# Sums of the down projection's weights: formed in DRAM during gate and up instead of in SBUF during the down projection

## The chip, the cores and the metric

The kernel runs on one core of a Trainium2 chip. The metric is the device time of one execution in microseconds (us), the median of several runs.

## The reference, cut to what matters

Two layers of a diffusion backbone. 640 tokens (512 latent, 128 context) of width 1024 pass a token mixer and a dense channel mixer. The stages concerned are the channel mixer's:

```python
def swiglu(h, w_gate_up, w_down):
    g, u = jnp.split(h @ w_gate_up, 2, axis=-1)
    return (jax.nn.silu(g) * u) @ w_down
...
    h2 = rmsnorm(x, g_pre_ffn) * (1.0 + scale2) + shift2
    x = x + gate2 * rmsnorm(swiglu(h2, w_gate_up, w_down), g_post_ffn)
```

`w_gate_up` is 1024 x 5632 and `w_down` 2816 x 1024 per layer, all float32. The modulation vectors (`scale`, `shift`, `gate`) come from `silu(c) @ w_ada`.

## The kernel before, in words

Every float32 matmul is made as three matmuls of rounded parts (`mm3`, L225): an operand is split into a high part by ScalarE (L211) and a low part by VectorE (L217), and high x high, high x low and low x high are summed in PSUM. So each block of weights is loaded to a `raw` buffer (three of them, 512 KB each), split by both engines into a `w` buffer (eight of them, shared with other large tiles), and read by TensorE.

**Gate and up** (`gate_up`, L944) goes over 22 column blocks of 128 hidden channels. The first two (`plain`) are multiplied directly; for the other 20, `fast` uses seven products of a 2 x 2 scheme of Strassen's kind instead of eight, each of 4 x 3 matmuls of 320 columns. `prep` (L964), a generator, loads the next block's two halves (L969), forms four sums of quarters on VectorE and splits seven operands; one step of it is made after each product of the current block. The results stand in six `hid` tiles.

**The down projection** (`w_down`, L1045) does the same with seven products over the contraction, in the order p1, p2, p5, p6, p3, p7, p4. Each goes over six groups of hidden channels (five of two 128-row blocks, one of one), so 11 blocks per product, with three accumulators of 512 columns (p1, p2, p3, p7) or two (p5, p6, p4). One group's weights are 512 KB. With (e, h) for the quarter of the weights, p1 uses (0,0), p2 (1,0), p3 (1,1), and the others sums: p5 (0,0)+(0,1); p6 that plus (1,1); p4 that plus (1,0); p7 (0,1)+(1,1). The sums are made by transfers that add into SBUF (`add`, L1078, issued by GpSimd): p1 loads into three `wk` tiles `V` (`into`, L1073), splits, then adds (0,1); p5 splits and adds (1,1); p6 splits and adds (1,0); p4 splits. p7 loads a fresh `raw` (`fresh`, L1081), adds to it and splits:

```python
        def p7(g):
            r = fresh(g, 0, 1)
            add(r, 1, 1, g)
            w = wsplit(g, r)
```

`run` (L1108) makes the operands of group g + 1 before the matmuls of group g. Pieces of the ends of earlier products (`later`: copies of accumulators to `cc`, `finish`, `end`) are put between the groups. In p7 and p4 the last two groups are run accumulator by accumulator (`tail=2`).

**The order of the work.** The program is written as one stream; each engine and each DMA queue (SP's, GpSimd's) works through its own instructions in the order of that stream as a scheduler lays it out, and waits on semaphores. A clock `now` counts TensorE's time while the program is built: `spawn` and `part` place delayed pieces by it, and `bg` holds background steps, one each time that the interval written with it has passed (`clk`, L160). In layer 0's gate and up the background is `queue_ada_w` (L383): the next layer's first modulation, 32 VectorE steps over 8 loads of 1 MB into `wk` tiles, one every 6.6 us. In layer 1's there is none.

Of the kernel before, what the change touches and what calls it, by code (L numbers as in the profile page):

```python
# [10 lines left out]
F32 = mybir.dt.float32  # L11
R = mybir.dt.float32r
AF = mybir.ActivationFunctionType
ALU = mybir.AluOpType
# [5 lines left out]
NJ = FF // 128  # L20
NPLAIN = 2
# [110 lines left out]
class Trunk:  # L132
# [250 lines left out]
    def queue_ada_w(self, l, r):  # L383


        nc, src = self.nc, self.a["ada"][3 * l + r - 1]
        mod, mc = self.new_mod(l, r)
        order = [(half, kk) for half in range(2) for kk in range(4)]
        box, raws = {}, []

        def fetch():
            if order:
                half, kk = order.pop(0)
                raw = self.W()
                nc.sync.dma_start(out=raw[:].rearrange("p (e n) -> p e n", e=2),
                                  in_=src[2 * kk : 2 * kk + 2, :, half * 1024 : half * 1024 + 1024].rearrange("e p n -> p e n"))
                raws.append(raw)

        def step(half, k, s):
            if k == 0 and s == 0:  # L400
                box["acc"] = self.wp.tile([128, 2, 1024], F32, tag="w", name=self.nm("acc"))
            if k % 2 == 0 and s == 0:
                box["raw"] = raws.pop(0)
                fetch()
            acc, raw = box["acc"], box["raw"][:, (k % 2) * 1024 : (k % 2) * 1024 + 1024]
            c = self.cond[:, k, s : s + 1]
            if k == 0:
                nc.vector.tensor_scalar(acc[:, s], raw, c, None, op0=ALU.mult)
            else:
                nc.vector.scalar_tensor_tensor(acc[:, s], raw, c, acc[:, s], op0=ALU.mult, op1=ALU.add)  # L410
            if k == 7 and s == 1:
                self.spawn(self.ada_sum(mod, mc, half, acc, 4.0), 5.66)

        return mod, [fetch] + [lambda h=h, k=k, s=s: step(h, k, s) for h in range(2) for k in range(8) for s in range(2)]

# [528 lines left out]
    def gate_up(self, l, pre):  # L944
        nc, a, blk = self.nc, self.a, self.blk
        hid = [self.Q([4, N], F32, "hid") for i in range(NJ // 4)]

# [5 lines left out]
        def plain(j, ws, c):  # L953
# [8 lines left out]
            out(j, c, pu[:, 0:320], s[:], nc.vector)  # L962

        def prep(j, ops):  # L964

            raws = []
            for u in range(2):
                raws.append(self.raw())
                nc.sync.dma_start(out=raws[u], in_=a["w_gu"][l, j, u])  # L969
            r = [x[:].rearrange("p (k i n) -> p k i n", k=4, i=2) for x in raws]  # L970
            (a11, a21), (a12, a22) = [[x[:, :, i, :] for i in range(2)] for x in r]
            g = [self.gp.tile([128, 2, 4, 128], F32, tag="gg", name=self.nm("sw")) for _ in range(2)]
            (s1, s2), (s3, s4) = [[x[:, i] for i in range(2)] for x in g]
            sums = {1: (s1, a21, a22, ALU.add), 2: (s2, s1, a11, ALU.subtract), 3: (s4, a12, s2, ALU.subtract), 4: (s3, a11, a21, ALU.subtract)}
            w = None
            for i, s in enumerate((a11, s1, s2, s4, s3, a12, a22)):
                if i % 2 == 0:
                    w = self.wp.tile([128, 2, 2, 4, 128], R, tag="w", name=self.nm("w"))
                if i in sums:
                    self.tt(*sums[i])  # L980
                op = [w[:, x, i % 2] for x in range(2)]
                self.split(op[0], op[1], s)
                ops.append(op)
                yield

        def fast(j, ops, nxt):
# [34 lines left out]
            product(C, a12, blk[1][0], True, g11)  # L1021
            product(A, a22, t4, False, lambda: out(j, 0, A, g0, nc.vector))

        ws = [[self.load(a["w_gu"][l, j, u]) for u in range(2)] for j in range(NPLAIN)]
        self.join(*pre[:3])
        for j in range(NPLAIN):
            plain(j, ws[j], 0)
        self.join(*pre)
        self.t_sums(256, 64)
# [4 lines left out]
        for j in range(NPLAIN):  # L1034
            plain(j, ws[j], 1)
            for _ in range(8):
                next(nxt, None)
# [6 lines left out]

    def w_down(self, l, src, hid, gg, nxt):  # L1045

# [11 lines left out]
        dd = [self.Q([3, 2, 384], F32, "dd") for _ in range(2)]  # L1058
        V = [None] * 3

# [8 lines left out]

        def vg(g):  # L1070
            return V[g // 2][:, (g % 2) * 1024 : (g % 2) * 1024 + cnt(g) * 512]

        def into(g, e, h):  # L1073
            if V[g // 2] is None:
                V[g // 2] = self.W()
            nc.sync.dma_start(out=vg(g), in_=dram(e, h, g))

        def add(dst, e, h, g):  # L1078
            nc.gpsimd.dma_start(out=dst, in_=dram(e, h, g), accum_op=ALU.add)

        def fresh(g, e, h):  # L1081
            r = self.raw()[:, 0 : cnt(g) * 512]
            nc.sync.dma_start(out=r, in_=dram(e, h, g))
            return r

        def wsplit(g, s):
            w = self.wp.tile([128, 2, 1024], R, tag="w", name=self.nm("w"))
            n = cnt(g) * 512
            self.split(w[:, 0, :n], w[:, 1, :n], s)
            return w  # L1090
# [85 lines left out]
        def p1(g):  # L1176
            into(g, 0, 0)
            w = wsplit(g, vg(g))
            add(vg(g), 0, 1, g)
            h = xsplit(g, [x(g, 0)[:, :, A4]])  # L1180
            self.tt(d(g), x(g, 1)[:, :, D4], x(g, 0)[:, :, D4], ALU.subtract)
            return h, w
# [6 lines left out]
        def p2(g):  # L1189
            w = wsplit(g, fresh(g, 1, 0))  # L1190
            return xsplit(g, [x(g, 1)[:, :, A4]]), w
# [13 lines left out]
        def p5(g):  # L1205
            w = wsplit(g, vg(g))
            add(vg(g), 1, 1, g)
            return xsplit(g, [d(g)[:, :, 128:384]]), w
# [5 lines left out]
        def p6(g):  # L1214
            w = wsplit(g, vg(g))
            add(vg(g), 1, 0, g)
            s = d(g)[:, :, 128:384]
# [8 lines left out]
        def p3(g):  # L1226
            w = wsplit(g, fresh(g, 1, 1))
            s = d(g)[:, :, 128:384]
# [8 lines left out]
        def p7(g):  # L1237
            r = fresh(g, 0, 1)
            add(r, 1, 1, g)
            w = wsplit(g, r)  # L1240
            h = self.Q([2, 2, 384], R, "hs")
# [7 lines left out]
        def p4(g):  # L1249
            return xsplit(g, [x(g, 1)[:, :, B4]]), wsplit(g, vg(g))  # L1250

# [90 lines left out]
    def run(self):  # L1342
# [4 lines left out]
        for l in range(L):  # L1347
# [8 lines left out]
            pre = self.w_out(l, src, x, ys, gg, mod2, last)  # L1356
            nxt = None
            if l + 1 < L:
                mod1, q = self.queue_ada_w(l + 1, 0)
                self.bg, self.bg_last = [(6.6, f) for f in q], self.now + 12.0  # L1360
            hid = self.gate_up(l, pre)
            self.drain_bg()
            gg = self.gates(gate, 1)
            if l + 1 < L:
                h = self.new_h()
                src = self.dp.tile([NT, 128, D], F32, tag="xs", name=self.nm("xs"))
                nxt = (mod1, h, src)
            pre = self.w_down(l, x, hid, gg, nxt)
            if l + 1 < L:
# [41 lines left out]
```

## Time and profile before

| | us |
|---|---|
| median of 3 runs (1386.08 to 1392.72) | 1387.79 |
| the profiled execution's own time | 1396.39 |
| its span in the profile | 1394.5 |
| TensorE busy in the span | 1342.1 |
| VectorE busy | 1023.3 |
| ScalarE busy | 692.0 |
| GpSimd busy | 151.3 |

Busy time of TensorE counts a matmul from start to a modelled end, and matmuls overlap; the distance of the starts tells its rate better. DMA-issuing instructions are not counted as busy. The granted clock of TensorE was 0.992 of full speed over the span. In the views, PE is TensorE, DVE VectorE, ACT ScalarE, POOL GpSimd and SP the engine that issues the plain transfers; `ps` is a tile in PSUM, `hs` the split activations of the down projection.

### The profile page before, as it was taken

Reading aid. Unit: us, or ns where it says so; the run is one execution under the profiler, and the core shown is the slowest. Engines: PE = TensorE matmul, PEld = TensorE weight load, DVE = VectorE, ACT = ScalarE, POOL = GpSimd, SP = SyncE. Lnnn points to the kernel's source line nnn. Section 1 sums busy time; section 2 is a strip of 40 time slices with the busy share of each in tenths; the row PEclk is TensorE's granted clock in tenths of the full one; section 3 lists DMA queues with packets and bytes.
Section 4 is the critical chain, followed back from the end, with each engine's and each line's share of the span. In section 5 each row is a group of like instructions: output and inputs, shape, how many; then the busy total and the mean of one; then the engine's idle time right before and its main releaser. Section 6 shows DMA issues by size and latency. Waiting matters only on the chain.

```text
span 1394.5 us, 21421 instructions
## 1 busy us (share of the span) xinstructions
PE 1342.1 (96%) x8188; PEld 1206.2 (86%) x8188; DVE 1023.3 (73%) x1794; ACT 692.0 (50%) x1398; POOL 151.3 (11%) x186
## 2 busy tenths in 40 slices
PE   5899999999999999999899999999999999999996
PEld 2788977899999999888688998878999999998875
DVE  3789476499988985776788956757977777675955
ACT  4543275465554554545583324746644544444633
POOL 1101121110000000111211101302000000010220
PEclk9999999999999999999999999999999999999998
DMA  9555247244333333768655533553222322375982
GB/s 373 168 166 184 82 147 241 99 146 143 125 108 106 120 121 110 194 139 192 183 181 184 186 112 121 176 204 124 73 92 91 90 78 85 98 184 126 183 211 97
DMA packets 57974, 203.68 MB, mean 146 GB/s; under 512 B 7488, under 2 KB 8384, under 8 KB 56848
## 3 DMA queue, kind: packets, MB, share of 16 engines
q1 hardware_dynamic: 50960, 179.25, 38.7%
q0 software_dynamic: 6912, 23.07, 9.4%
q8 instruction: 64, 1.05, 0.3%
q14 instruction: 38, 0.31, 0.1%
HBM read 191.61 MB, written 10.68 MB: 145 GB/s over the span
## 4 chain that ended last, share of the span: by engine, by line
PE 71%; DMA 9%; DVE 8%; issue 5%; ACT 4%; POOL 2%; POOLq 0%; DVEq 0%; SPq 0%; ACTq 0%
PE ps L227 22%; PE ps L229 22%; PE ps L228 22%; DMA raw<-in_w_dn 4%; PE ps L240 2%; DVE w L217 2%; DVE acc L377 2%; PE ps L284 2%; ACT w L211 2%; DMA raw<-in_w_out 1%; PE ps L829 1%; POOL rt L252 1%; DMA raw<-in_ada 1%; DMA raw<-in_w_vpc 1%; DMA raw<-in_w_b 1%
## 5 line engine op out<-in xcount | busy, mean ns | idle before, releaser
L217 DVE TENSOR_TENSOR w<-raw,w 128x512 fp32r<-128x512 f32 (+2 forms) x220 | 197.5, 903 | 105.5 <-ACT w L211 104.0
L211 ACT ACTIVATE w<-raw 128x512 fp32r<-128x512 f32 (+2 forms) x220 | 175.4, 801 | 185.5 <-PE ps L229 74.8
L227 PE MATMUL ps<-T,w 128*128 128x320 f32 x640 | 198.5, 310 | 0.0
L229 PE MATMUL ps<-T,w 128*128 128x320 f32 x640 | 197.8, 309 | 0.0
L228 PE MATMUL ps<-T,w 128*128 128x320 f32 x640 | 197.7, 309 | 0.0
L227 PE MATMUL ps<-b,w 128*128 128x320 f32 x608 | 188.1, 309 | 0.0
L228 PE MATMUL ps<-b,w 128*128 128x320 f32 x608 | 187.9, 309 | 0.0
L229 PE MATMUL ps<-b,w 128*128 128x320 f32 x608 | 187.9, 309 | 0.0
L227 PE MATMUL ps<-w,hs 128*128 128x512 f32 x396 | 156.7, 396 | 6.6 <-ACT cc L211 4.6
L229 PE MATMUL ps<-w,hs 128*128 128x512 f32 x396 | 156.4, 395 | 5.5 <-DVE hs L217 5.4
L228 PE MATMUL ps<-w,hs 128*128 128x512 f32 x396 | 156.3, 395 | 0.2 <-DVE w L217 0.2
L211 ACT ACTIVATE w<-sw 128x512 fp32r<-128x512 f32 x160 | 96.3, 625 | 77.3 <-PE ps L229 65.3
L211 ACT ACTIVATE s<-ps 128x320 f32<-128x320 f32 (+2 forms) x148 | 65.3, 443 | 129.1 <-PE ps L229 105.9
L214 DVE TENSOR_TENSOR s<-ps,s 128x320 f32<-128x320 f32 (+1 forms) x144 | 68.7, 482 | 80.1 <-PE ps L229 79.9
L227 PEld LDWEIGHTS ps<-T,w 128*128 128x128 f32 x640 | 120.1, 188 | 2.1 <-issue 1.7
L228 PEld LDWEIGHTS ps<-T,w 128*128 128x128 f32 x640 | 120.1, 188 | 0.0
L229 PEld LDWEIGHTS ps<-T,w 128*128 128x128 f32 x640 | 120.1, 188 | 0.0
L227 PEld LDWEIGHTS ps<-b,w 128*128 128x128 f32 x608 | 114.1, 188 | 0.4 <-ACT s L211 0.3
L228 PEld LDWEIGHTS ps<-b,w 128*128 128x128 f32 x608 | 114.1, 188 | 0.1
L229 PEld LDWEIGHTS ps<-b,w 128*128 128x128 f32 x608 | 114.1, 188 | 0.0
L217 DVE TENSOR_TENSOR w<-sw,w 128x512 fp32r<-128x512 f32 x160 | 106.2, 686 | 5.1 <-ACT w L211 3.1
L227 PEld LDWEIGHTS ps<-w,hs 128*128 128x128 f32 x396 | 75.6, 191 | 23.8 <-ACT cc L211 5.4
(236 smaller groups left out, 2856.3 us busy)
## 6 DMA issues: line engine op xcount, KB each, us to landing
raw<-in_w_gu SPq DMA_DIRECT2D x88, 512.0 KB, 3.5
raw<-in_ada SPq DMA_DIRECT2D x64, 512.0 KB, 4.3
raw<-in_w_dn SPq DMA_DIRECT2D x30, 512.0 KB, 4.3
wk<-in_w_dn POOLq DMA_DIRECT2D x30, 512.0 KB, 6.2
ada<-in_ada SPq DMA_DIRECT2D x8, 1024.0 KB, 15.5
raw<-in_w_out SPq DMA_DIRECT2D x16, 512.0 KB, 4.1
wk<-in_ada SPq DMA_DIRECT2D x8, 1024.0 KB
xs<-work SPq DMA_DIRECT2D x15, 512.0 KB, 4.6
```

Source lines behind the costliest of these rows:

```text
L211: self.nc.scalar.activation(out, in_, f, **kw)
L214: self.nc.vector.tensor_tensor(out, x, y, op=op)
L217: self.nc.vector.tensor_tensor(lo, src, hi.bitcast(F32), op=ALU.subtract)
L227: mm(out, lh, rh, start=start, stop=False, skip_group_check=more)
L228: mm(out, lh, rl, start=False, stop=False, skip_group_check=more)
L229: mm(out, ll, rh, start=False, stop=stop, skip_group_check=more)
L240: self.nc.tensor.transpose(out, in_, self.ident)
L252: self.nc.gpsimd.tensor_tensor(r2, r, self.mhalf[:, :n], op=ALU.pow)
L284: self.nc.tensor.matmul(ps[32 * j : 32 * j + 32, :], self.cond[:, k, :], s, start=start, stop=stop, tile_position=(0, 32 * j))
L377: nc.vector.scalar_tensor_tensor(acc[:, s], raw, c, acc[:, s], op0=ALU.mult, op1=ALU.add)
L829: self.nc.tensor.matmul(ps[64 * e : 64 * e + 64, :], lhs[e], rhs[e], start=start, stop=stop, tile_position=(0, 64 * e))
```

## The change

The four sums of the down projection's weights are formed in DRAM, in 24 new tiles (four sums, six groups), by copying and adding transfers that GpSimd issues while gate and up runs: 36 background steps per layer with 24 copies and 24 adds. Before each step GpSimd copies one element per partition of the newest finished `hid` column (`self.pace`), and the step's transfers are ordered behind that copy. In layer 0 the steps are mixed with those of `queue_ada_w`, two after each three of these, 69 in 215 us by the build-time clock; in layer 1 they are alone, 36 in 215 us. In the down projection all seven products load their weights into `raw` through SP. Gate and up loads a block's two halves into one `w` buffer, one block earlier than before; `queue_ada_w` loads halves of 512 KB into `raw`, two ahead.

```diff
     def queue_ada_w(self, l, r):
...
-        order = [(half, kk) for half in range(2) for kk in range(4)]
+        order = [(half, k) for half in range(2) for k in range(8)]
...
-                half, kk = order.pop(0)
-                raw = self.W()
-                nc.sync.dma_start(out=raw[:].rearrange("p (e n) -> p e n", e=2),
-                                  in_=src[2 * kk : 2 * kk + 2, :, half * 1024 : half * 1024 + 1024].rearrange("e p n -> p e n"))
-                raws.append(raw)
+                half, k = order.pop(0)
+                raws.append(self.raw())
+                nc.sync.dma_start(out=raws[-1], in_=src[k][:, half * 1024 : half * 1024 + 1024])
...
-        return mod, [fetch] + [lambda h=h, k=k, s=s: step(h, k, s) for h in range(2) for k in range(8) for s in range(2)]
+        return mod, [lambda: [fetch(), fetch()]] + [lambda h=h, k=k, s=s: step(h, k, s) for h in range(2) for k in range(8) for s in range(2)]
...
     def gate_up(self, l, pre):
         nc, a, blk = self.nc, self.a, self.blk
+        self.pace = None
...
+        raws = {}
+
+        def fetch(j):
+
+            if j < NJ:
+                raws[j] = self.W()
+                for u in range(2):
+                    nc.sync.dma_start(out=raws[j][:, u * 1024 : u * 1024 + 1024], in_=a["w_gu"][l, j, u])
+
         def prep(j, ops):
 
-            raws = []
-            for u in range(2):
-                raws.append(self.raw())
-                nc.sync.dma_start(out=raws[u], in_=a["w_gu"][l, j, u])
-            r = [x[:].rearrange("p (k i n) -> p k i n", k=4, i=2) for x in raws]
+            fetch(j + 1)
+            r = raws.pop(j)[:].rearrange("p (u k i n) -> p u k i n", u=2, k=4, i=2)
+            r = [r[:, u] for u in range(2)]
...
             product(A, a22, t4, False, lambda: out(j, 0, A, g0, nc.vector))
+            self.pace = hid[j // 4][:, j % 4, 0:1]
...
             plain(j, ws[j], 0)
+        fetch(NPLAIN)
...
             plain(j, ws[j], 1)
+            self.pace = hid[0][:, j, 639:640]
...
+    def queue_sums(self, l):
+
+
+        nc, a = self.nc, self.a
+        v = [[self.dp.tile([128, 1040], F32, tag=f"v{i}{g}", name=self.nm("v"))[:, 0 : (2 if g < 5 else 1) * 512] for g in range(6)] for i in range(4)]
...
+        def copy(i, g, s):
+            nc.gpsimd.dma_start(out=v[i][g], in_=s)
+
+        def add(i, e, h, g):
+            nc.gpsimd.dma_start(out=v[i][g], in_=dram(e, h, g), accum_op=ALU.add)
+
+        def paced(f):
+
+            def go():
+                t = self.M([1], "pace", 2)
+                ins = nc.gpsimd.tensor_copy(t, self.pace)
+                with self.tc.issue_after(ins.ins):
+                    f()
+            return go
+
+        todo = []
+        for g in range(6):
+            todo.append(lambda g=g: [copy(0, g, dram(0, 0, g)), copy(2, g, dram(0, 1, g))])
+        for g in range(6):
+            todo.append(lambda g=g: [add(0, 0, 1, g), add(2, 1, 1, g)])
+        for i, (e, h) in ((1, (1, 1)), (3, (1, 0))):
+            for g in range(6):
+                todo.append(lambda g=g, i=i: copy(i, g, v[0 if i == 1 else 1][g]))
+            for g in range(6):
+                todo.append(lambda g=g, i=i, e=e, h=h: add(i, e, h, g))
+        return v, [paced(f) for f in todo]
+
-    def w_down(self, l, src, hid, gg, nxt):
+    def w_down(self, l, src, hid, gg, vs, nxt):
...
-        def wsplit(g, s):
+        def wsplit(g, src):
+            s = self.raw()[:, 0 : cnt(g) * 512]
+            nc.sync.dma_start(out=s, in_=src)
...
         def p1(g):
-            into(g, 0, 0)
-            w = wsplit(g, vg(g))
-            add(vg(g), 0, 1, g)
+            w = wsplit(g, dram(0, 0, g))
...
         def p5(g):
-            w = wsplit(g, vg(g))
-            add(vg(g), 1, 1, g)
+            w = wsplit(g, vs[0][g])
...
         def p7(g):
-            r = fresh(g, 0, 1)
-            add(r, 1, 1, g)
-            w = wsplit(g, r)
+            w = wsplit(g, vs[2][g])
...
         def p4(g):
-            return xsplit(g, [x(g, 1)[:, :, B4]]), wsplit(g, vg(g))
+            return xsplit(g, [x(g, 1)[:, :, B4]]), wsplit(g, vs[3][g])
...
             pre = self.w_out(l, src, x, ys, gg, mod2, last)
             nxt = None
+            vs, qs = self.queue_sums(l)
             if l + 1 < L:
                 mod1, q = self.queue_ada_w(l + 1, 0)
-                self.bg, self.bg_last = [(6.6, f) for f in q], self.now + 12.0
+                both = []
+                while q or qs:
+                    both += q[:3] + qs[:2]
+                    q, qs = q[3:], qs[2:]
+                qs = both
+            self.bg, self.bg_last = [(215.0 / len(qs), f) for f in qs], self.now + 30.0
```

(p2, p3 and p6 change in the same way: `wsplit` of (1,0), of (1,1) and of `vs[1]`.)

## Rows read from the trace of the kernel before

**Rows 1.** Windows of gate and up: window, its length, busy us (xinstructions) PE, PEld, DVE, ACT, POOL; clock, DMA share, GB/s.
```profile
315.00:330.00 15.00, 15.00 (x105) 15.00 (x104) 15.00 (x25) 8.50 (x17) 0.00 (x0) 1.00 0.27 93
1040.00:1190.00 150.00, 150.00 (x1025) 150.00 (x1024) 109.09 (x195) 73.61 (x147) 0.00 (x0) 1.00 0.28 88
```

**Rows 2.** Windows, down projection's matmuls (`hs`) alone: window, length, PE busy (xmatmuls), clock, DMA share, GB/s.
```profile
560.00:719.20 159.20, 139.68 (x594) 0.98 0.73 177
690.00:700.00 10.00, 8.45 (x25) 0.69 0.10 33
```

**Rows 3.** Timeline of TensorE: a fed stretch's ends, then each down projection's first and last start.
```profile
1309.79 0.39 PE L228 MATMUL ps<-w,hs 128*128 128x512 f32 x1
...
1342.88 0.39 PE L227 MATMUL ps<-w,hs 128*128 128x512 f32 x1
...
568.43 0.39 PE L227 MATMUL ps<-w,hs 128*128 128x512 f32 x1
...
716.15 0.39 PE L229 MATMUL ps<-w,hs 128*128 128x512 f32 x1
...
1242.89 0.39 PE L227 MATMUL ps<-w,hs 128*128 128x512 f32 x1
...
1386.79 0.39 PE L229 MATMUL ps<-w,hs 128*128 128x512 f32 x1
```

**Rows 4.** Groups by line of TensorE, 568.4 to 716.3 us: the transposes.
```profile
L240 PE MATMUL ps<-ident,work 128*128 128x128 f32 x24 | 2.9, 272 | 0.0
```

**Rows 5.** Timeline of TensorE, late in both down projections: start, us, instruction, [idle before <-releaser].
```profile
687.86 0.50 PE L229 MATMUL ps<-w,hs 128*128 128x512 f32 x1 [2.75 <-DVE hs L217]
...
690.78 0.79 PE L229 MATMUL ps<-w,hs 128*128 128x512 f32 x1 [1.22 <-DVE hs L217]
...
696.34 0.40 PE L227 MATMUL ps<-w,hs 128*128 128x512 f32 x1
...
1367.46 0.50 PE L227 MATMUL ps<-w,hs 128*128 128x512 f32 x1 [2.84 <-ACT cc L211]
```

**Rows 6.** Waits, 640 to 716 and 1320 to 1390 us: total, times, longest us.
```profile
ACT w L211 <- DMA raw<-in_w_dn: 17.9, 4, 8.4
...
PE ps L227 <- ACT cc L211: 4.6, 2, 2.8
```

**Rows 7.** Transfers: `in_w_dn`'s GpSimd issues and landing; `in_w_gu`'s; `raw` 560 to 720; layer 1.
```profile
L1079 POOL DMA_DIRECT2D wk<-in_w_dn x30: 853/873/1085, 559.1 to 1310.1; - x30
...
DMA to landing us min/median/max: 3.3/6.2/9.5
...
DMA to landing us min/median/max: 3.4/3.5/5.7
...
DMA to landing us min/median/max: 3.3/4.2/5.2
...
raw<-in_w_dn SPq DMA_DIRECT2D x13, 512.0 KB, 6.1
```

**Rows 8.** Groups by line and shape, 1240 to 1395 us: weight splits; count, busy us, mean ns, idle before.
```profile
L217 DVE TENSOR_TENSOR w<-raw,w 128x1024 fp32r<-128x1024 f32 x15 | 18.4, 1225 | 22.3 <-ACT w L211 22.2
...
L211 ACT ACTIVATE w<-raw 128x1024 fp32r<-128x1024 f32 x15 | 15.9, 1057 | 27.2 <-DMA raw<-in_w_dn 17.5 <-PE ps L229 7.4 <-issue 2.3
```

**Rows 9.** DMA queues (packets, MB, share): 557 to 700 us, then 284 to 557, 960 to 1215.
```profile
q0 software_dynamic: 3456, 11.54, 45.2%
q1 hardware_dynamic: 4073, 13.24, 29.0%
...
q1 hardware_dynamic: 8906, 32.92, 37.0%
...
q1 hardware_dynamic: 6480, 23.60, 29.4%
```

**Rows 10.** Tile `acc`, VectorE in layer 0's gate and up: duration ns min/median/max, first and last start.
```profile
L410 DVE SCALAR_TENSOR_TENSOR acc<-wk,cond,acc x28: 1276/1279/1285, 322.9 to 509.6; 128x1024 f32<-128x1024 f32 x28
```

**Rows 11.** Timeline of GpSimd, down projection of layer 1.
```profile
1352.20 0.73 POOL L248 TENSOR_SCALAR rs<-mso 128x1 f32<-128x1 f32 x1 [0.34 <-ACT work L211]
```

More of the change, by code (lines that the diff above doesn't have):

```diff
@@ L401, in step @@
                 box["acc"] = self.wp.tile([128, 2, 1024], F32, tag="w", name=self.nm("acc"))
-            if k % 2 == 0 and s == 0:
+            if s == 0:
                 box["raw"] = raws.pop(0)
                 fetch()
-            acc, raw = box["acc"], box["raw"][:, (k % 2) * 1024 : (k % 2) * 1024 + 1024]
+            acc, raw = box["acc"], box["raw"]
             c = self.cond[:, k, s : s + 1]
@@ L1043, in gate_up, with dram @@
         return hid
-    def w_down(self, l, src, hid, gg, nxt):
+    def queue_sums(self, l):
+        nc, a = self.nc, self.a
+        v = [[self.dp.tile([128, 1040], F32, tag=f"v{i}{g}", name=self.nm("v"))[:, 0 : (2 if g < 5 else 1) * 512] for g in range(6)] for i in range(4)]
+        def dram(e, h, g):
+            return a["w_dn"][l, e, h, g] if g < 5 else a["w_dt"][l, e, h]
+        def copy(i, g, s):
[21 more added lines that the diff above has]
+    def w_down(self, l, src, hid, gg, vs, nxt):
         a, nc = self.a, self.nc
@@ L1058, in w_down @@
         dd = [self.Q([3, 2, 384], F32, "dd") for _ in range(2)]
-        V = [None] * 3
         def x(g, e):
@@ L1068, in dram @@
             return a["w_dn"][l, e, h, g] if g < 5 else a["w_dt"][l, e, h]
[L1070 to L1084, printed above, removed]
-        def wsplit(g, s):
+        def wsplit(g, src):
+            s = self.raw()[:, 0 : cnt(g) * 512]
+            nc.sync.dma_start(out=s, in_=src)
             w = self.wp.tile([128, 2, 1024], R, tag="w", name=self.nm("w"))
@@ L1189, in p2 @@
         def p2(g):
-            w = wsplit(g, fresh(g, 1, 0))
+            w = wsplit(g, dram(1, 0, g))
             return xsplit(g, [x(g, 1)[:, :, A4]]), w
@@ L1214, in p6 @@
         def p6(g):
-            w = wsplit(g, vg(g))
-            add(vg(g), 1, 0, g)
+            w = wsplit(g, vs[1][g])
             s = d(g)[:, :, 128:384]
@@ L1226, in p3 @@
         def p3(g):
-            w = wsplit(g, fresh(g, 1, 1))
+            w = wsplit(g, dram(1, 1, g))
             s = d(g)[:, :, 128:384]
@@ L1367, in run @@
                 nxt = (mod1, h, src)
-            pre = self.w_down(l, x, hid, gg, nxt)
+            pre = self.w_down(l, x, hid, gg, vs, nxt)
             if l + 1 < L:
```

## The prediction

> **What bounds the kernel now.** I read the windows first. In gate and up (layer 0 about 284 to 568 us, layer 1 about 960 to 1243) TensorE is busy all the time at the full granted clock: 1025 matmuls of 320 columns in 150 us, one per 0.146 us, with the DMA engines a third busy and GpSimd idle [rows 1]. No wait of TensorE shows there, so nothing done for these matmuls can shorten that stage; it can only be harmed. One block of 84 matmuls lasts 84 x 0.146 = 12.2 us.
>
> The down projection is the other stage the change touches. It has 594 matmuls of 512 columns per layer [rows 2]. Where TensorE is fed, they start every 0.2266 us: 146 steps between the two starts shown, 33.09 us [rows 3]. 594 of them need 134.6 us. From the first start to the last, and one step more, layer 0 takes 716.15 - 568.43 + 0.23 = 147.9 us and layer 1 1386.79 - 1242.89 + 0.23 = 144.1 us [rows 3]. In layer 0 24 transposes lie in between, 2.9 us [rows 4]. **What is lost: 10.4 us in layer 0, 9.5 in layer 1, together 19.9 us.**
>
> It is lost late. The starts stand still before 687.86, 690.78 and 1367.46, and after such a halt 13 matmuls run at a slow step: from 690.78 to 696.34 they take 5.56 us where 2.95 would do [rows 5], a step of 0.43 us, the lower of the clock's two levels (1.2 GHz instead of 2.4), and the granted clock of that 10 us window is 0.69 [rows 2]. Idle engine first, lower clock behind it: 2.6 us of each layer's loss are this echo, and go if the halt goes.
>
> What ends the waits: ScalarE's split of a weight block waited 17.9 us for `raw<-in_w_dn` in the last part of layer 0, 8.4 us at one time [rows 6]. That is the seventh product, p7 (L1237): each of its six blocks is loaded through SP, then added to by a second transfer that GpSimd may issue only when the first has landed, and then split. One load lands in 3.3 to 5.2 us; transfers of this weight with the adds among them take up to 9.5 [rows 7]. Load and add together outlast the 18 x 0.2266 = 4.1 us that TensorE needs per block of p7. ScalarE's queue is held by that wait, so the copies of sums (`cc`) behind it come late, and TensorE waits for them too: 4.6 us in layer 1 [rows 6].
>
> **The change, part by part.** Removed from each down projection: 24 adding transfers on GpSimd's queue and the add in front of each split in p7. From p7's path goes the second transfer; what is late next there is a single load, 3.3 to 5.2 us with two more raw buffers in flight, under 4.1 us a block. I take the waits, the slow clock behind them and the late `cc` copies as gone, but leave 2 us per layer for what is not tied to the add (the copies of accumulators before p4, the `hs` operands behind other work). Gain 19.9 - 4 = **16 us**; bounds 0 (another wait fills the gap) and 19.9.
>
> Added to each down projection: 18 more loads through SP (p5, p6, p4 formerly split sums that already lay in SBUF). All 42 now go through three raw buffers. In the two-accumulator phases a block lasts 12 x 0.2266 = 2.72 us. A buffer's cycle is landing 4.2, ScalarE's split 1.06, VectorE's 1.23 [rows 8], and by my estimate 0.6 to 1.5 behind another split: 7.1 to 8.0, a third of it 2.4 to 2.7 us. It just fits, and p2 and p3 (4.1 us a block) leave the buffers full at its start, so I take 0. With the 6.1 us landing seen in layer 1 beside the adds [rows 7] it would be 3.0 to 3.3 us; that is the other end, a rival below. SP's queue holds the loads behind the stores and reloads of x; a store waiting for its sum would hold them, but in the trace p7's loads stand ahead of it.
>
> Moved into each gate and up: 24 adds and 24 copies, DRAM to DRAM, 11.5 MB each kind. The trace has no transfer from DRAM to DRAM. An add into SBUF is its nearest row: 11.54 MB took 45.2% of 143 us, 64.6 us of all 16 engines; plain loads took 29.0% for 13.24 MB, 3.1 us per MB [rows 9]. So adds cost 65 (as into SBUF) to 129 us (twice, the target lying in DRAM as well), copies 36 (as a load) to 65 (as an add): 101 to 194 us. I take 120, nearer the lower end, the same operations on the same queue. The Trainium skill (DMA: Bandwidth & Descriptors, Latency and other measured facts) states 214 GB/s per direction for copies between HBM tensors; by it the copies are an estimated 54 us, which no run here shows, and the sum would be 119. The engines have 37.0% of 273 us, 101 us, of other work in layer 0 and 29.4% of 255 us, 75 us, in layer 1 [rows 9]. With 120 more they are 81% and 76% full. TensorE feels this only through late weights, and those are now asked for a block, 12.2 us, ahead; alone they land in 3.4 to 5.7 us [rows 7]. Cost 0 with that cover; without it, the slower rival.
>
> GpSimd also gets 36 one-element copies and 48 issues of about 0.87 us [rows 7] per layer, some 42 us on an engine with no other work in that stage; they wait for `hid`, and only later sums stand behind them. No ScalarE or VectorE work is added. But in layer 0 the modulation steps come every 3.116 x 5 / 3 = 5.2 us instead of 6.6. For 171 us VectorE then has 72.7% (layer 1's own load, 109.09 of 150 us) x 171 + 32 x 1.28 = 165 us of work, 97% [rows 1, 10]. From 315 to 330 us it was busy all the time and TensorE with it [rows 1], so 0 to 3 us; I take 0. Weights already there also remove VectorE's own waits for them.
>
> **Sum.** -16 us against the profiled execution's own 1396.39: 1380.4. That execution is 8.6 us above the median of the runs, 1387.79. Stages that TensorE bounds should hardly vary, so a part of the 8.6 may sit in the very waits that go, which no row shows; carried over unchanged the median becomes **1372 us**.
>
> **The rivals.**
> *Loads take the place of the adds.* Three raw buffers pace p5, p6 and p4 at up to 3.3 us a block. 17 blocks x 0.3 to 0.6 us are 5 to 10 us per layer given back: 1382, up to 1388. For it: the cycle just fits. Against: the 6.1 us landing was measured beside adds that are gone, and DMA work of layer 0's stage falls from 64.6 + 41.5 = 106 us to 41.5 + 18 loads of 8.7 MB in all x 3.1 = 69 us.
>
> *Slower: the sums stand in the weights' way.* At the upper price the engines have 295 us of work in 273, and 269 in 255: 22 and 14 us too much. If the sums are served first, the weights of gate and up come late by this and TensorE stops: 1372 + 36 = 1408; half of it, 1390. It decides once both loads of a block need over 12.2 us. For it: weight landings rose from 3.5 to 4.2 and 6.1 us beside adds [rows 7]. Against: even the worst transfer shown, 9.5 us, is below 12.2. The Trainium skill says that transfers issued by different engines run on the same 16 DMA engines and interleave (DMA: Bandwidth & Descriptors, Issuing engines are not separate DMA queues); the risen landings agree.
>
> *The pacing copies hold VectorE.* A one-element GpSimd operation shows 0.73 us [rows 11]. If VectorE stood still for each of the 22 copies in layer 0's 171 us, 16 us join 165, 10 too much: 1382. This is a rule of the Trainium skill (SBUF — State Buffer, Who interferes with whom): a VectorE operation with two SBUF inputs contends with a GpSimd operation that reads SBUF. No row shows VectorE slowed by it.
>
> *The change doesn't do what it says*: the sums are unfinished when p5 to p4 ask for them, and SP waits. At the end of gate and up 0 to 36 us of them may be left, but the last sum is read some 100 us later; 1388.
>
> *The surplus was in the waits*: unprofiled, the halts were smaller by up to 8.6 us: 1380.
>
> **How the numbers follow.** About 0.5%, 7 us, is what a measurement of this kernel can tell from no change. Forecast (1364 to 1379) 0.62; loads instead of adds 0.12, half of it beyond the bound; sums in the way 0.11, slower; pacing copies 0.05, about at the bound; sums unfinished 0.05, the same; surplus 0.05, at the bound. Faster 0.74, same 0.15, slower 0.11. The range, 1364 (the whole 19.9 us and a little of the runs' own spread) to 1388, leaves out the slower rival and tails of the rest.
>
> **What would show it.** Right: the 594 matmuls of each down projection in 135 to 140 us, no clock under 1.0 in the last third, no wait of ScalarE for `raw` above 2 us, weights of gate and up landing in 4 to 8 us with TensorE still at 1025 per 150 us. Wrong: fewer than 1015 matmuls in 150 us of gate and up; VectorE waiting for the weights there; SP waiting for GpSimd's transfers; or splits in p5, p6 and p4 that wait for `raw` at each block.

## The result, and the profile after

The changed kernel takes **1375.27 us** (median of 4 runs, 1373.93 to 1376.86) against 1387.05 of the kernel before on the same chip (4 runs, 1386.08 to 1392.72): ratio 0.9900, 95% interval 0.9872 to 0.9927, so 10.1 to 17.8 us less. The forecast was 1372, its range 1364 to 1388. In a later series the same kernel came out at 0.9913 (0.9884 to 0.9942).

The profiled execution took 1373.93 us. From its page, the span, the busy time of each engine, the DMA queues and the issues from DRAM to DRAM (`v`):

```profile
span 1372.2 us, 21590 instructions
...
PE 1331.6 (97%) x8188; PEld 1200.3 (87%) x8188; DVE 1031.7 (75%) x1794; ACT 694.4 (51%) x1398; POOL 218.5 (16%) x306
...
q1 hardware_dynamic: 56272, 196.56, 42.6%
q0 software_dynamic: 13312, 46.14, 14.3%
...
v<-in_w_dn POOLq DMA_DIRECT2D x60, 512.0 KB, 7.3
...
v<-v POOLq DMA_DIRECT2D x20, 512.0 KB, 5.0
```

GpSimd's queue q0 now moves 46.14 MB, 14.3% of 16 engines over 1372.2 us: 196 us of the time of all 16 engines, 98 per layer.

The timeline of TensorE, first and last start of each down projection, to be laid beside [rows 3]:

```profile
565.66 0.39 PE L227 MATMUL ps<-w,hs 128*128 128x512 f32 x1
...
703.27 0.39 PE L229 MATMUL ps<-w,hs 128*128 128x512 f32 x1
...
1229.89 0.39 PE L227 MATMUL ps<-w,hs 128*128 128x512 f32 x1
...
1364.34 0.39 PE L229 MATMUL ps<-w,hs 128*128 128x512 f32 x1
```

Layer 0 takes 137.61 us from first to last start (147.72 before), layer 1 134.45 (143.90): 10.1 and 9.5 us less, **19.6 together**. Fed without a halt, 593 steps of 0.2266 us are 134.4; with layer 0's 2.9 us of transposes [rows 4] 137.3. So 0.3 us is left of the halts. The windows of the `hs` matmuls agree: window, length, TensorE's busy time and count, granted clock, DMA share, GB/s. Late in each stage the clock is full, where [rows 2] had 0.69:

```profile
670.00:700.00 30.00, 28.41 (x124) 1.00 0.61 190
...
1330.00:1364.00 34.00, 34.00 (x152) 1.00 0.43 148
```

The waits (total, times, longest us), first 565 to 704 us, then 1229 to 1372:

```profile
ACT w L211 <- DMA raw<-in_w_dn: 5.4, 4, 2.2
...
ACT w L211 <- DMA raw<-in_w_dn: 7.5, 4, 3.2
```

ScalarE waited 17.9 us for `raw<-in_w_dn` in the last 76 us of layer 0's stage alone [rows 6]; now 5.4 in all of it (and 2.2 for the smaller `raw<-in_w_dt`), and TensorE's long wait for `cc` is gone. No split waits for a sum (`raw<-v`). One load lands in these times (tile `raw`, the same two stretches):

```profile
DMA to landing us min/median/max: 2.9/3.3/3.6
...
DMA to landing us min/median/max: 3.4/3.9/5.6
```

Gate and up, in the columns of [rows 1]:

```profile
315.00:330.00 15.00, 14.50 (x99) 14.22 (x98) 15.00 (x26) 7.50 (x15) 0.48 (x1) 1.00 0.31 105
1040.00:1190.00 150.00, 149.25 (x1015) 148.72 (x1015) 112.89 (x194) 72.98 (x144) 29.82 (x50) 1.00 0.68 178
```

1015 matmuls instead of 1025 in 150 us, with the DMA engines 68% busy instead of 28%. Over the whole stage, first gate/up start to first `hs` start, that is 281.1 us for 279.1 in layer 0 and 276.7 for 275.8 in layer 1.

So the two profiled executions differ like this: down projections -19.6, gate and up +3.0, stages that the change doesn't touch -5.7; spans 1394.5 and 1372.2, 22.3 less. The medians differ by 11.8. What stands between is below.

### The profile page after: what moved, and what is told of

The parts are those of the page before. It is cut to its first block, busy times and chain, and to the rows that moved or that the text cites. A ratio compares the mean times of both kernels' runs of the same rounds, so it can differ in the third digit from the quotient of the medians.

```text
span 1372.2 us, 21590 instructions
## 1 busy us (share of the span) xinstructions
PE 1331.6 (97%) x8188; PEld 1200.3 (87%) x8188; DVE 1031.7 (75%) x1794; ACT 694.4 (51%) x1398; POOL 218.5 (16%) x306
## 3 DMA queue, kind: packets, MB, share of 16 engines
q0 software_dynamic: 13312, 46.14, 14.3%
## 5 line engine op out<-in xcount | busy, mean ns | idle before, releaser
L211 ACT ACTIVATE w<-raw 128x1024 fp32r<-128x1024 f32 (+3 forms) x148 | 147.1, 1000 | 95.1 <-DMA raw<-in_w_b 39.6
L217 DVE TENSOR_TENSOR w<-raw,w 128x1024 fp32r<-128x1024 f32 (+3 forms) x148 | 170.4, 1155 | 29.9 <-ACT w L211 29.4
L227 PE MATMUL ps<-w,hs 128*128 128x512 f32 x396 | 154.4, 390 | 0.1
L228 PE MATMUL ps<-w,hs 128*128 128x512 f32 x396 | 154.1, 389 | 0.0
L229 PE MATMUL ps<-w,hs 128*128 128x512 f32 x396 | 153.9, 389 | 0.0
L211 ACT ACTIVATE w<-wk 128x512 fp32r<-128x512 f32 x120 | 74.9, 628 | 107.0 <-PE ps L229 97.1
## 6 DMA issues: line engine op xcount, KB each, us to landing
ada<-in_ada SPq DMA_DIRECT2D x8, 1024.0 KB, 11.9
```

What stands on the lines that cost most here:

```text
L211: self.nc.scalar.activation(out, in_, f, **kw)
L217: self.nc.vector.tensor_tensor(lo, src, hi.bitcast(F32), op=ALU.subtract)
L227: mm(out, lh, rh, start=start, stop=False, skip_group_check=more)
L228: mm(out, lh, rl, start=False, stop=False, skip_group_check=more)
L229: mm(out, ll, rh, start=False, stop=stop, skip_group_check=more)
```

## The experiments

**Theory**: the gain is p7's load-then-add and nothing else; the other 36 of a layer's 48 transfers give back what they bring, and the lead of the weights only makes room for them. **Rivals**: moving the other sums gains too; the lead alone gains; the halts vary from run to run; the sums cost time in gate and up.

The experiments ran in three series, each with runs of the kernel before. Stage lengths are read as above, in one profiled execution of each kernel; "ahead" is all before the first gate/up matmul of layer 0, "between" from the last `hs` start of layer 0 to layer 1's gate and up. They leave out some 8 us at the end.

| kernel | median us | ratio to before (95%) | ahead | gate/up 0 | down 0 | between | gate/up 1 | down 1 |
|---|---|---|---|---|---|---|---|---|
| before | 1387.05 | | 289.3 | 279.1 | 147.7 | 251.0 | 275.8 | 143.9 |
| before again | 1391.59, one run | | 289.0 | 279.4 | 146.3 | 246.8 | 275.8 | 144.8 |
| changed | 1375.27 | 0.9900 (0.9872-0.9927) | 284.5 | 281.1 | 137.6 | 249.9 | 276.7 | 134.5 |
| changed again | 1374.94 | 0.9913 (0.9884-0.9942) | 284.3 | 279.8 | 137.6 | 250.8 | 276.7 | 134.4 |
| no add in p7 | 1371.81 | 0.9880 (0.9849-0.9911) | 283.6 | 280.5 | 138.2 | 246.5 | 276.1 | 134.4 |
| p7's sum only | 1372.65 | 0.9883 (0.9850-0.9915) | 287.7 | 277.4 | 139.9 | 249.6 | 275.4 | 134.4 |
| the same again | 1372.35 | 0.9894 (0.9869-0.9920) | 284.6 | 277.3 | 139.8 | 246.7 | 275.7 | 134.4 |
| p7's sum, no lead | 1374.57 | 0.9874 (0.9850-0.9898) | 284.6 | 279.8 | 139.9 | 246.3 | 276.1 | 134.4 |
| p7's add on VectorE | 1376.70 | 0.9890 (0.9864-0.9917) | 287.6 | 279.0 | 140.2 | 251.2 | 275.9 | 134.9 |
| lead only | 1391.16 | 1.0019 (1.0000-1.0038) | 286.8 | 281.4 | 145.3 | 245.2 | 275.7 | 140.1 |
| sums, no lead | 1404.38 | 1.0114 (1.0083-1.0145) | 286.2 | 293.8 | 137.6 | 251.1 | 294.5 | 134.4 |
| sums doubled | 1441.61 | 1.0383 (1.0353-1.0414) | 285.6 | 313.2 | 137.7 | 246.2 | 306.8 | 134.4 |
| pacing copies x8 | 1383.53 | 0.9938 (0.9917-0.9959) | 289.5 | 284.5 | 137.6 | 247.0 | 282.1 | 134.4 |
| no pacing | 1470.22 | 1.0563 (1.0538-1.0587) | 386.7 | 279.9 | 137.6 | 249.0 | 275.4 | 134.4 |

The untouched stages first: "ahead" spreads from 283.6 to 289.5 and "between" from 245.2 to 251.2, "no pacing" aside. Two profiles of one kernel lie up to 3.1 us apart "ahead" (p7's sum only) and 4.1 "between" (before); the kernel before and the one without p7's add, whose code is the same up to there, lie 5.8 apart "ahead". One such difference shows in the clock: TensorE was granted 0.77 of full speed in the first 30 us of the first profile of p7's sum only, and 1.00 in the second. So these stages differ by 3 to 6 us between executions; what a kernel does is read from the down projections and from gate and up.

### The kernel before, again

No edit.

> The kernel before, unchanged, profiled a second time. Theory (the halts of the down projection differ from execution to execution, and the first profile, 1396.39 us, had more of them than the timed runs, median 1387): own time 1386 to 1390, the two down projections lose 10 to 14 us together against 594 x 0.2266 us each, instead of 19.9, and the stretch ahead of layer 0's gate and up is shorter than the 289.3 us of the first profile by some us. Rival (the halts are fixed, and the change gives 8 us back elsewhere): they lose 19 to 21 us again.

The down projections took 146.3 and 144.8 us, 19.4 more than halt-free, and not the 10 to 14 of the theory on record. The loss that the prediction read is no accident of its one execution.

### The changed kernel, again

No edit.

> The changed kernel unchanged, timed in the same series as the next three and the kernel before. Theory (the 19 to 20 us of halts go, and gate and up and the stages the change does not touch vary by some us from run to run): 14 to 18 us faster than the kernel before in this series. Rival (the sums' transfers cost something in gate and up that the profile hides): 10 to 13 us.

0.9913 (0.9884 to 0.9942), and every stage of the two layers within 1.4 us of its first profile: the down projections are halt-free again.

### p7 without its add

In the kernel before:

```diff
 r = fresh(g, 0, 1)
-add(r, 1, 1, g)
```

> The kernel before with the adding transfer in p7 left out, so p7 multiplies (0,1) alone; nothing else differs, no sum is made in DRAM. Theory (p7's load and add in a row is the whole loss): down projections of 134.5 to 138 us between first and last start, as in the changed kernel, and a time within 3 us of the changed kernel's 1375. Rival (the changed kernel gives something back in gate and up): 1367 to 1371, clearly below the changed kernel. Other rival (the adds of p1, p5 and p6 cost as well): 1379 to 1383.

0.9880: all that the change gains, and the stages down to 138.2 and 134.4, with the 18 other adds of a layer still there, SBUF as their target, and no lead. p7's second transfer is the loss but for 0.9 us in layer 0; in layer 1 not even a tenth of a microsecond is left.

### Only p7's sum in DRAM

The changed kernel with the w_down of before, but p7's blocks from DRAM; 12 paced transfers per layer instead of 48. Run in two series.

```diff
-todo.append(lambda g=g: [copy(0, g, dram(0, 0, g)), copy(2, g, dram(0, 1, g))])
+todo.append(lambda g=g: copy(2, g, dram(0, 1, g)))
...
-todo.append(lambda g=g: [add(0, 0, 1, g), add(2, 1, 1, g)])
+todo.append(lambda g=g: add(2, 1, 1, g))
...
-r = fresh(g, 0, 1)
-add(r, 1, 1, g)
+r = self.raw()[:, 0 : cnt(g) * 512]
+nc.sync.dma_start(out=r, in_=vs[2][g])
```

> The changed gate and up, but only p7's sum made in DRAM (6 copies and 6 adds per layer instead of 24 and 24); the other three sums in SBUF as before. Theory: same time as the changed kernel, 1373 to 1377, since only p7's add was on the path. Rival (the other adds slow the loads of p2, p3 and p7): 1379 to 1384, with ScalarE waiting for raw in p7.

> p7's sum alone in DRAM, the other three in SBUF, with the lead of a block in gate and up: the kernel of e3 again, for a comparison within one series. Theory (36 of the 48 transfers in DRAM bring nothing): within 2 us of the changed kernel. Rival (they cost something in gate and up): 2 to 5 us faster than the changed kernel, 16 to 20 us faster than before.

0.9883 and 0.9894. Down 0 keeps 2.3 us that the changed kernel loses (139.9 for 137.6), gate and up is 3.5 to 5.0 us shorter (both layers, against the two profiles of the changed kernel). The other 36 transfers of a layer bring 2.3 us and cost as much or more. In the series with both, this kernel is 2.6 us below the changed one, but their intervals overlap: not told apart.

### p7's sum without the lead

The same, with the weight loads and `queue_ada_w` of the kernel before (no `fetch` a block ahead).

> p7's sum alone in DRAM (12 transfers per layer), gate and up's weights and the modulation loaded as in the kernel before, without the lead of a block. Theory (the harm grows with the number of transfers: 48 without the lead made 1404, 48 with it 1375, 96 with it 1442): 12 without the lead cost little, 1372 to 1380. Rival (any transfer beside loads without the lead stops TensorE): 1385 to 1395.

0.9874. For 12 transfers a layer the lead is not needed. The profile of its layer 0, 285 to 565 us, q0 (packets, MB, share) and TensorE's wait for the operand sums (`s`):

```profile
q0 software_dynamic: 1818, 6.33, 11.0%
...
PE ps L227 <- DVE s L214: 0.9, 2, 0.5
```

### p7's add on VectorE

No sum in DRAM at all; p7 loads both summands through SP, and VectorE adds:

```diff
 r = fresh(g, 0, 1)
-add(r, 1, 1, g)
+r2 = fresh(g, 1, 1)
+self.tt(r, r, r2, ALU.add)
```

> The kernel before, but p7 loads both summands through SP into two raw buffers and VectorE adds them; no adding transfer in p7 and none in DRAM. Theory (three raw buffers hold one and a half blocks, a cycle of 4.2 + 1.2 + 1.1 + 1.2 us per block pair): p7 still halts a little, 2 to 8 us lost per layer in the down projection instead of 9.5, time 1375 to 1385. Rival (VectorE's queue, busy with p7's splits, takes the place of the transfer): 1386 or more.

0.9890, from a change of two lines. Its waits from 640 to 715 us:

```profile
ACT w L211 <- DVE raw L214: 10.1, 5, 3.2
...
PE ps L227 <- ACT hs L211: 1.6, 1, 1.6
```

The split still waits 10.1 us, now for the add, but TensorE 1.6. The second summand is still loaded for every block, so what cost the time in the kernel before was not its bytes. It was the adding transfer behind the load: that it starts only when the load has landed, and that it takes longer than a load (7.9 us for 3.3, shown below); no run separates the two.

### The lead alone

The kernel before with the changed `queue_ada_w` and the changed loads of gate and up; no sums.

> Only the loads of gate and up one block ahead (and the modulation's 512 KB loads into raw); the down projection as before, no sum in DRAM. Theory: TensorE has no wait in gate and up to lose, so the time is that of the kernel before, within 3 us, with the down projections 144 to 147 us from first to last start. Rival (the lead is worth something by itself): 5 us or more faster than before.

1.0019 (1.0000 to 1.0038): the lead brings nothing by itself. Its waits, 640 to 715 us and then 1300 to 1376:

```profile
POOL raw L1087 <- DMA raw<-in_w_dn: 23.1, 3, 14.3
...
ACT w L211 <- DMA raw<-in_w_dn: 14.7, 5, 4.3
...
ACT w L211 <- DMA raw<-in_w_dn: 14.2, 5, 3.7
...
PE ps L227 <- ACT cc L211: 3.7, 2, 1.9
```

The first line is the chain itself: GpSimd's add stands waiting for the load of the same block, and ScalarE for both. (The longest of these waits, 14.3, lies ahead of p7's first add, where GpSimd has nothing else to do; it costs nothing.) Yet this execution lost 13.7 us in the down projections (285.4 less the halt-free 271.7), not 19.4, and layer 1's stage, 140.1, is shorter than the 144 to 147 expected. What makes the same chain cost less in one execution was not traced.

### The sums without the lead

The changed kernel with the loads of gate and up and of `queue_ada_w` as before.

> All four sums in DRAM, but gate and up loads its weights as before (a block's halves into raw when its preparation begins), and the modulation too (1 MB into w buffers). Theory (the lead of a block covers the transfers that the sums delay): VectorE waits for raw in gate and up, TensorE stops there, 3 to 12 us slower than the changed kernel, 1378 to 1387. Rival (the buffers' own slack is cover enough): within 2 us of the changed kernel.

1.0114, slower than before, though the down projections are as short as in the changed kernel. Gate and up is 12.7 and 17.8 us longer, where 3 to 12 in all were expected. The waits in layer 0, 300 to 560 us, and one halt in the timeline of TensorE:

```profile
DVE sw L214 <- DMA raw<-in_w_gu: 20.3, 12, 3.7
...
PE ps L227 <- DVE s L214: 8.2, 4, 5.8
```

```profile
434.49 0.63 PE L227 MATMUL ps<-T,w 128*128 128x320 f32 x1 [5.79 <-DVE s L214]
```

VectorE's weight sums (`sw`) wait for weights; behind them in its queue stand the operand sums `s`, which TensorE then lacks. The lead is worth 28 us (1.0114 less 0.9913, times 1388), but only because of the 48 transfers.

### Twice the sums

The changed kernel, each copy and add issued a second time into an array that nobody reads:

```diff
 nc.gpsimd.dma_start(out=v[i][g], in_=s)
+nc.gpsimd.dma_start(out=v[i + 4][g], in_=s)
...
 nc.gpsimd.dma_start(out=v[i][g], in_=dram(e, h, g), accum_op=ALU.add)
+nc.gpsimd.dma_start(out=v[i + 4][g], in_=dram(e, h, g), accum_op=ALU.add)
```

> The changed kernel with every copy and add of the sums made twice, the second time into tiles that nothing reads: 96 transfers per layer instead of 48. Theory (the sums share the 16 DMA engines with the weights, and a block of lead covers the present number with room left): the software queue's share in gate and up doubles from 33%, the weights' landing rises from 4.5 to 6 to 9 us, TensorE begins to wait, 0 to 10 us slower than the changed kernel. Rival (the cover is at its limit already): 20 to 40 us slower. Other rival (the transfers hardly meet): within 1 us.

66.7 us above the changed kernel of its series, more than theory (0 to 10) and rival (20 to 40) allowed. In the changed kernel and then here, DMA queues 285 to 565 us, and the landing of `in_w_gu` (of the loads of both layers, the profile shows the landing of 10 in each kernel):

```profile
q1 hardware_dynamic: 9136, 33.10, 34.1%
q0 software_dynamic: 6316, 22.14, 32.0%
...
DMA to landing us min/median/max: 3.5/4.5/7.7
```

```profile
q0 software_dynamic: 10892, 37.95, 53.6%
q1 hardware_dynamic: 8484, 30.89, 30.7%
...
PE ps L227 <- DVE s L214: 16.8, 8, 4.3
...
DMA to landing us min/median/max: 4.2/5.8/12.1
```

At 66% of the engines (62% in layer 1) weights land in 4.5 us and TensorE hardly notices; at 84% in both layers, with a sixth of the engines' time still free, single loads take up to 12.1 us and gate and up grows by 32 and 30 us. A part of that is the clock behind the halts: 0.96 and 0.97 granted in the two stages, where the changed kernel has 1.00.

### Eight pacing copies for one

```diff
-ins = nc.gpsimd.tensor_copy(t, self.pace)
+for _ in range(8):
+    ins = nc.gpsimd.tensor_copy(t, self.pace)
```

> The changed kernel with eight pacing copies in place of each one, 288 per layer. Theory (the copies wait on GpSimd and hold nothing else; VectorE's operations on two SBUF inputs keep their 0.685 us): within 3 us of the changed kernel, 1372 to 1379. Rival (GpSimd's reads hold VectorE): 252 more copies of 0.2 to 0.7 us per layer stand in VectorE's way, at least 10 us slower in layer 0, 1385 or more, and VectorE's sums longer than 0.70 us in the mean.

0.9938: 3 to 5 us of the gain given back by the ratios, more than the 3 expected at most; in its profile gate and up is 3.4 to 4.7 us longer in layer 0 and 5.3 in layer 1. The copies (tile `pace`; ns min/median/max), the sums (groups of VectorE's line 214, 300 to 560 us: count, busy us, mean ns, idle before) and the landing of `in_w_gu`:

```profile
L1073 POOL COPY pace<-hid x528: 177/184/6597, 334.0 to 1218.6; 128x1 f32<-128x1 f32 x176
...
L214 DVE TENSOR_TENSOR sw<-wk 128x512 f32<-128x512 f32 x38 | 26.2, 691 | 10.7 <-DMA wk<-in_w_gu 10.7
...
DMA to landing us min/median/max: 3.9/6.6/9.0
```

VectorE's sums take 691 ns; in the changed kernel they take this:

```profile
L214 DVE TENSOR_TENSOR sw<-wk 128x512 f32<-128x512 f32 x37 | 25.2, 684 | 2.0 <-DMA wk<-in_w_gu 2.0
```

Eight times the copies lengthen VectorE's work by 1%. What grew is its wait for weights, 2.0 to 10.7 us, and 11.9 to 21.6 in layer 1, as they land later. Why the same transfers delay them more here wasn't settled; that they leave GpSimd in tighter bunches is a guess.

### No pacing

```diff
-t = self.M([1], "pace", 2)
-ins = nc.gpsimd.tensor_copy(t, self.pace)
-with self.tc.issue_after(ins.ins):
-    f()
+f()
```

> The changed kernel without the pacing copies and the order behind them: GpSimd issues the sums' transfers as early as it can. Theory (too many transfers at a time delay the weights by more than the lead): bursts at the begin of gate and up, landings above 12 us, 10 to 60 us slower than the changed kernel. Rival (pacing is not needed since the queues take turns): within 3 us of the changed kernel.

Slower by 5.6%: GpSimd issues all 96 transfers, of both layers, from 1.2 us on, and they meet the loads of the first stages. "Ahead" takes 386.7 us, some 100 more, where 10 to 60 in all were expected. Windows of that stretch (columns of [rows 1]), then the queues from 0 to 285 us and from 0 to 31, where nearly all that q0 carries are copies:

```profile
0.00:100.00 100.00, 45.22 (x217) 30.28 (x217) 26.52 (x66) 29.33 (x57) 27.80 (x49) 0.85 1.01 327
...
100.00:200.00 100.00, 64.49 (x310) 55.90 (x311) 48.35 (x74) 20.57 (x56) 33.00 (x51) 0.81 1.04 288
```

```profile
q0 software_dynamic: 13312, 46.14, 63.7%
...
q0 software_dynamic: 1245, 4.58, 37.5%
```

The DMA engines are full, TensorE is busy half of the time, and its granted clock is 0.81 to 0.85, a mean between the two levels (0.5 and 1.0 of 2.4 GHz). The run also prices the sums: 63.7% of 285 us is 182 us for 46.14 MB, 91 per layer; the copies of the first 31 us took 11.6 us for 4.58 MB, 2.5 us per MB. And with the sums out of it, gate and up takes 279.9 and 275.4 us: paced beside it (281.1 and 279.8, 276.7 both times) they cost 0 to 1.2 us in layer 0 and 1.3 in layer 1.

## Why the prediction was right, and where it was off

**What is lost, and why: right.** 19.9 us was read off the starts of the `hs` matmuls, put down to p7's load and then add, and its echo in the clock. Without p7's add alone the stages fall to their halt-free lengths but for 0.9 us, and in the changed kernel the granted clock there is 1.00. The prediction set load and add of one block against the 4.1 us that TensorE needs; but three blocks are in flight in three buffers, so a third of a buffer's cycle is what counts. Here are p7's loads and adds in the kernel before, DMA issues 640 to 716 us, median us to landing last:

```profile
raw<-in_w_dn SPq DMA_DIRECT2D x6, 512.0 KB, 3.3
raw<-in_w_dn POOLq DMA_DIRECT2D x5, 512.0 KB, 7.9
```

The adds take over twice as long as the load (whose 3.3 is a single landing; the last three loads of p7 went out 5.7 to 6.5 us before the adds that waited for them). By the starts on SP's queue, each of the three buffers was loaded again 15.4, 16.1 and 17.1 us after its last load: a block every 5.1 to 5.7 us, too slow for 4.1. So the conclusion stands.

**"Leave 2 us per layer": too much caution.** It was kept for `cc` copies and `hs` operands behind other work. Those were late because ScalarE's queue stood at p7's split: 19.6 us went, where 16 were taken, and 19.0 without p7's add alone.

**Loads through three raw buffers at 0: right.** The cycle was reckoned with landings of 4.2 us; they are 3.3 and 3.9, and the slow 6.1 belonged to the adds, as the rival's counter-argument said. ScalarE waits 5.4 and 7.5 us for `raw<-in_w_dn`, up to 3.2 at once, above the 2 named as a limit; these are loads of p1 to p3, the sums of p5 to p4 are not waited for, and TensorE doesn't halt. The rival in which loads take the place of the adds fell.

**Sums in DRAM, 120 us per layer out of 101 to 194: too dear.** 98 beside gate and up, 91 without pacing, both below the lower bound. That bound took a copy as a plain load, 3.1 us per MB, and an add into DRAM as one into SBUF, 5.6 [rows 9]. The changed kernel shows each kind alone in its second layer, queue q0 from 990 to 1033 us (12 copies) and from 1033 to 1071 (12 adds):

```profile
q0 software_dynamic: 1600, 5.77, 39.7%
...
q0 software_dynamic: 1728, 5.77, 81.7%
```

That is 17.1 and 31.0 us, 3.0 us per MB for the copies and 5.4 for the adds; later stretches of that stage give 3.3 to 3.4 and 5.9 to 6.0. Both rows were the right ones; what was mis-sized is the step from their sum, 101, up to 120, for a dearer target in DRAM, of which nothing shows. The rate that the prediction quoted from the Trainium skill (DMA: Bandwidth & Descriptors, Latency and other measured facts), 54 us for the copies of a layer, is above their engine time here, 3.0 x 11.5 = 34 us.

**The cover, "asked for a block, 12.2 us, ahead": mis-sized.** In the changed kernel, the timeline of SP's queue and of VectorE, one block's load and its first use:

```profile
428.72 0.81 SPq L969 DMA_DIRECT2D wk<-in_w_gu  x2
```

```profile
435.62 0.69 DVE L214 TENSOR_TENSOR sw<-wk 128x512 f32<-128x512 f32 x1 [0.78 <-DMA wk<-in_w_gu]
```

6.9 us, not 12.2, and VectorE already waited 0.78 of it. Over all blocks it is 4.9 to 14.8 us, in the median 6.5 in layer 0 and 5.8 in layer 1. The load is written a block ahead but can't be issued there, for a buffer must come free (the waits of SP's queue, 320 to 545 us):

```profile
SPq L969 <- DVE w L217: 105.1, 12, 11.5
```

Nor was the kernel before without any lead: there a block's second load left 4.1 us before the block's first use (median of either layer), in the changed kernel 6.1 and 5.4. So what the change adds is 1.3 to 2.0 us. One sign that the prediction was to be wrong by did show, though it cost TensorE little, and the 1015 matmuls stand right at another: VectorE waited for weights, 2.0 us in layer 0 and more in layer 1 (953 to 1230 us):

```profile
DVE sw L214 <- DMA wk<-in_w_gu: 11.9, 5, 3.6
```

So the point at which the slower rival decides lies lower than the prediction put it. Its mechanism is real: without the lead it makes the kernel 1.1% slower, with twice the sums 3.8%, at engine loads of 63 and 84% (285 to 565 us), not past 100% as that rival reckoned. It didn't come here because the sums cost 98 us where its upper price was 194, and because some 6 us are nearly enough at 62 to 66%.

**Gate and up at 0: off by about a microsecond per layer**, 0.4 to 2.0 us in layer 0 and 0.9 to 1.0 in layer 1 (first and second profiles of both kernels). VectorE in layer 0 was full in the 15 us window and TensorE lost 6 of 105 matmuls there; the 0 to 3 us that the prediction allowed holds it.

**Pacing copies at 0: right.** What eight times as many cost was a wait for weights, not the one that the rival named. They last 0.2 to 6.6 us on GpSimd, while VectorE's sums keep their 0.684 us (0.691 beside eight times as many). The rule quoted from the Trainium skill (SBUF — State Buffer, Who interferes with whom) names a contention; the wait that these runs show is GpSimd's, not VectorE's.

**The profiled execution and the median: the weak step.** 1380.4 less the whole 8.6 us was taken, with a rival at 0.05 that the surplus sat in the halts. By its stages the profiled pair gives 16.6 us for the touched ones (19.6 less 3.0), the medians 11.8 and 12.8, with intervals up to 17.8 and 16.1. Three things bear on it: the execution that the prediction read, 1396.39 us, is slower than each of the 39 timed runs of that kernel (1383.64 to 1395.63); untouched stages differ by 3 to 6 us between executions; and the halts differ too (19.9, 19.4, 13.7 us in three profiles without the sums; the last belongs to the fastest of its kernel's 12 runs, 1383.83 us). If an execution at the median has some 15 us of halts, all numbers meet. Halts in an unprofiled run can't be seen, so this stays open. And that the forecast's 16 us meet the profiled 16.6 is luck in part: the halts that went were 3.6 us more than taken, the cost in gate and up 3.0 us more. The rival of the surplus deserved more than 0.05.

**The open ends.** No version with as much gain is separated from the changed kernel by its interval. The plainest with the same gain is p7's add on VectorE, two lines, without DRAM sums, pacing or lead.

## What to carry to other kernels

Where an accumulating transfer follows the load of the same tile, its landing time comes on top of the load's; ask of each such pair whether its consumer has that much slack, and mend the one pair that hasn't before moving all. With several buffers in flight, compare the whole cycle of a buffer, divided by their number, with the time that the consumer needs per block. When transfers are moved under a stage that TensorE bounds, count the slack of that stage's own loads from the moment when their buffer comes free, not from where the code asks, and expect late loads well before the engines are full. A saving read from one execution is good to no more than stages differ between executions, so read a second one before carrying its surplus to the median.

## What the hardware showed that was not expected

- Adds from DRAM to DRAM took 5.4 us of 16 engines per MB, about as much as adds into SBUF (5.6 [rows 9]); copies took 3.0 (2.5 in the first 31 us of the kernel without pacing), about as much as plain loads (3.1).
- Weights came late in gate and up at 84% of the engines' time (longest landing 12.1 us, for 7.7 at 62 to 66%; 10 landings each).
- One-element copies on GpSimd beside VectorE's sums took between 0.18 and 6.6 us, and the sums no longer than before.
